# The second mixer's stick-breaking attention in single steps with stacked operands, and later turns at post-norms

## The chip, the cores and the metric

One Trainium2 chip, one of its cores. The metric is the device time of one execution in microseconds (us), as the median of the runs. On this kernel about 0.2% (7 us) can be told from no change.

## What is computed

A model of 512 tokens by 1024 features runs through two stacks in fp32. The first has two layers of a mixer (differential attention, retention, pooling) and a convolutional MLP; each result is normalised by a gain of its own ("post-norm") before it is added to x. The second has two layers of a gated MLP, a hybrid mixer (dilated windows and a stick-breaking attention) and another gated MLP. The parts that matter here:

```
x = x + rms_norm(mix, norm_mix_post[l]); h = rms_norm(x, norm_mlp_pre[l])   # post-norm
x = x + rms_norm(y, norm_mlp_post[l])                                       # post-norm

# stick-breaking attention, four heads of 64, q scaled by 1/8
z = q . k                                  # 512 x 512 a head, only keys before the query
log_keep = log_sigmoid(-z) = -softplus(z)
after = sum of log_keep over keys between this one and the query
o = exp(log_sigmoid(z) + after) . v

# dilated windows: 12 heads in 3 groups (dilation 1, 4, 16), rotary on q and k
```

## The kernel before

**Dense products.** Every weight is read from HBM in chunks of 128 x 1024 (`Stream`), split by ScalarE and VectorE into a high and a low fp32r part (L63, L64), and each product is three fp32r matmuls: high by high, high by low, low by high (`mm3a`, `mm3b`, L177 to L185). `fm` makes features by tokens, one 128 x 512 bank a chunk (24 matmuls); `tm` makes tokens by features in four banks at once, one for each tile of 128 tokens. With `halves`, `fm` first runs four chunks over tokens 0 to 255 and then over 256 to 511.

**Order by hand.** The program is emitted in one fixed order for each engine. Every dense step calls `tick`, which moves a clock on by 640 for three matmuls of 512 columns; the clock counts planned nanoseconds, not real ones. Three kinds of other work are put in by that clock. `later` queues steps of the norms with a due time and a token tile; `flush(t)` forces those of tiles up to t (an infinite due time leaves a step to that alone). `after` queues splits of rotated rows. `bg` holds generators (`stick`, then `dilated(0)`, then `dilated(1)`): each runs to its next `yield n` and then waits for n more ticks. `drain` runs what is left of them at once. Each engine takes its own instructions strictly in the order of emission, so one that waits holds up all behind it.

**Post-norms.** `finish` runs the last product of a stage in two halves of features. For a post-norm, `part1` (L340 to L358) takes ScalarE's square sum of a bank, multiplies the bank by its gain on VectorE (L347), makes the scale on GpSimd; `add`, 1200 ticks later, adds both halves to x (L354); then square sums of x, `rows_of_h` (2300 ticks later) scales x to xn on VectorE (L210), and `to_h` turns xn on TensorE into banks ph (L220) and splits them to h (L162, L163). `to_h` is due 1800 ticks after that, but for the last token tile, which waits for `flush`: in `fm` with halves at the start of the second half, in the first product of mix1 (`opens`) before tile t.

**Second mixer** (`mix2`, twice). In order: four half-run chunks make sq0, sk0, sq1, sk1 (two heads each); a `tm` makes v; six chunks q0, q2, q4, k0, k2, k4, each rotated (`rope`, L499 to L502: VectorE shuffle, VectorE multiply, GpSimd multiply, GpSimd add) and split 4500 ticks later; a second `tm` for the other v; six more chunks q1 to k5; sixteen gate chunks, with `drain` behind the twelfth. `stick` starts with the first `tm` and is followed by the two `dilated`, which wait for their names and 2500 ticks past the newest split. `stick` works on one head at a time: a mask and the scores into three banks z (plain fp32 matmuls on 64 rows, L1139 and L1140), softplus of the four blocks (three ScalarE functions, L1145 to L1147, and one VectorE step, L1148), splits, prefix sums over the keys by fp32r matmuls with triangles of -1 (`neg_tri`, L1157) and of blocks by all -1, exponentials, and the product with v (`pos`). Every helper `mm` records its matmuls at L1121. Its temporary tiles come from 9 buffers (`scr`), other features from 24 (`fm`).

Of the kernel before, what the change touches and what calls it, by code (L numbers as in the profile page):

```python
# [91 lines left out]
class Block:  # L92
# [225 lines left out]
    def finish(self, nk, rows, gain, scale=None, post=None, final=False):  # L318
# [21 lines left out]
        def part1(t, ps):  # L340
# [5 lines left out]
            self.square_sum(ys[t][:, 1:2], ps)  # L346
            nc.vector.tensor_mul(ps, ps, post[:, 512:])  # L347
            nc.gpsimd.tensor_add(ys[t][:, 2:3], ys[t][:, 0:1], ys[t][:, 1:2])
            self.rstd(ys[t][:, 3:4], ys[t][:, 2:3], D)

            def add():
                for n, src in ((0, y0[t]), (1, ps)):
                    x = self.X[:, t, n * 512:(n + 1) * 512]
                    nc.vector.scalar_tensor_tensor(x, src, ys[t][:, 3:4], x, op0=OP.mult, op1=OP.add)  # L354

                def sums():
                    self.x_ready(t, 0, ss[t])
                    normed(t)  # L358

                self.later(1900, t, sums)  # L360
# [3 lines left out]
        def normed(t):  # L364
# [3 lines left out]
            def rows_of_h():  # L368
                parts = self.scaled_rows(t, r, gain)
                if final:  # L370
                    for n in range(2):
                        nc.sync.dma_start(self.out[0, t * 128:(t + 1) * 128, n * 512:(n + 1) * 512], parts[n])
                else:
                    self.later(1800 if t < NT - 1 else math.inf, t, lambda: self.to_h(t, parts, first))

# [486 lines left out]
    def mix2(self, l, next_gain, final):  # L862
# [21 lines left out]
        def dil(name):  # L884
# [6 lines left out]
            def evac(ps):  # L891
# [3 lines left out]
                def split():  # L895
# [3 lines left out]
                    fm["at"] = self.clock  # L899
                self.after(4500, split)  # L900
            return evac
# [82 lines left out]
    def dilated(self, half, fm, v, o_dil):  # L984
# [6 lines left out]
        while any(n not in fm for n in names):  # L991
            yield 300
        while self.clock < fm["at"] + 2500 and not self.forced:
            yield 300
# [124 lines left out]
    def stick(self, fm, v, o_sb):  # L1119
# [4 lines left out]

        def split(x):
            n = x.shape[-1]
            hi = part()
            lo = hi[:, n:2 * n] if 2 * n <= T else part()[:, :n]
            self.split_to(hi[:, :n], lo, x)
            return hi[:, :n], lo  # L1130

        for h in range(4):
            c, s = divmod(h, 2)
            p = slice(64 * s, 64 * s + 64)
            q, k = fm[f"sq{c}"][p], fm[f"sk{c}"][p]
            banks = [self.bank(self.bg_tag, "pz") for _ in range(3)]
            z = [banks[0], banks[1][:, :384], banks[2][:, :256], banks[2][:, 256:384]]
            for b in range(NT):
                mm(z[b][:, :128], self.ident_bf, self.strict_kq, b < 3)  # L1139
                mm(z[b], k[:, b * 128:(b + 1) * 128], q[:, b * 128:], False)  # L1140
            x0, x1, x2 = [self.spare(f"sp{i}") for i in range(3)]
            sp = [x0, x1[:, :384], x2[:, :256], x1[:, 384:]]
            for b in range(NT):
                x = sp[b]
                nc.scalar.activation(x, z[b], AF.Abs)  # L1145
                nc.scalar.activation(x, x, AF.Exp, scale=-1.0)
                nc.scalar.activation(x, x, AF.Ln, bias=1.0)  # L1147
                nc.vector.scalar_tensor_tensor(x, z[b], 0.0, x, op0=OP.max, op1=OP.add)  # L1148
            yield 4500 if h else 6000
            parts = [split(sp[0]), split(sp[1]), split(sp[2])]  # L1150
            nc.vector.tensor_add(sp[2][:, 128:], sp[2][:, 128:], sp[3])
            nc.vector.tensor_add(sp[1][:, 128:], sp[1][:, 128:], sp[2])
            past = [split(sp[1]), split(sp[2])]
            yield 3500
            for b in range(3):
                for x in parts[b]:
                    mm(z[b], self.neg_tri, x, False)  # L1157
            mm(z[2][:, 128:], self.neg_ones.bitcast(F32), sp[3], False)
            mm(z[3], self.neg_tri.bitcast(F32), sp[3], False)
            yield 1000  # L1160
# [4 lines left out]
            for b in range(NT):  # L1165
# [3 lines left out]
                w.append(x[:, :n])  # L1169
            yield 4000  # L1170
            while ("v", NT - 1) not in fm:
# [158 lines left out]
```

## Time and profile before

| | us |
|---|---|
| median of 3 runs | 3435.41 |
| lowest, highest | 3434.85, 3436.55 |
| the profiled execution | 3436.64 |
| its span, first to last instruction | 3434.9 |
| TensorE busy (matmuls) | 3352.0 |
| VectorE busy | 1542.0 |
| ScalarE busy | 1192.8 |
| GpSimd busy | 356.3 |

The profile is of one execution. A matmul's end is modelled and overlaps the next one's start, so the distance from start to start tells what a matmul costs; busy time tells only that TensorE was not idle. The idle time in front of an instruction stands in square brackets in the timeline, with what ended it. The granted clock of TensorE (PEclk) is 1.00 at 2.4 GHz and 0.50 at 1.2 GHz; a window that is a little wider than a half-speed stretch shows 0.51.

### The profile page before, as it was taken

The numbers are of one execution on the slowest core, as the hardware profiler recorded it, in microseconds if no ns is written. First come the engines' busy times: TensorE is split into PE (matmuls) and PEld (weight loads), VectorE is DVE, ScalarE is ACT, GpSimd is POOL, SyncE is SP. The second block draws the span as 40 slices with busy tenths as digits, with TensorE's granted clock in tenths as the row PEclk, the third lists the DMA queues.
The fourth block names the chain that finished last, engine by engine and source line by source line (L and its number), as shares of the span: only waits on it lengthen the run. The fifth ranks groups of instructions, "written<-read, shape, count | busy, mean of one in ns | idle before, by whom it ended". The sixth has DMA issues, their size and how long they took to land.

```text
span 3434.9 us, 39516 instructions
## 1 busy us (share of the span) xinstructions
PE 3352.0 (98%) x16080; PEld 2770.5 (81%) x16080; DVE 1542.0 (45%) x2013; ACT 1192.8 (35%) x1886; POOL 356.3 (10%) x412
## 2 busy tenths in 40 slices
PE   8999999999999999999999999999999999999999
PEld 6778888767888888888688888888888878888887
DVE  4665542466555243323564533324332457453332
ACT  4344432434443232223533332223222443432222
POOL 2421110242110000000220100000000022010000
PEclk9999999999999999999999999999999999999999
DMA  4122332312233222232112232322232212223232
GB/s 158 49 75 86 104 112 92 108 50 75 86 105 111 92 93 96 95 104 97 59 64 77 90 103 95 104 92 97 95 104 98 96 51 68 82 91 103 94 103 80
DMA packets 87190, 311.99 MB, mean 91 GB/s; under 512 B 10368, under 2 KB 11072, under 8 KB 87008
## 3 DMA queue, kind: packets, MB, share of 16 engines
q1 hardware_dynamic: 85536, 305.17, 26.6%
q0 software_dynamic: 1472, 4.30, 0.4%
q8 instruction: 127, 2.08, 0.2%
q14 instruction: 55, 0.45, 0.0%
HBM read 307.32 MB, written 2.10 MB: 90 GB/s over the span
## 4 chain that ended last, share of the span: by engine, by line
PE 87%; DVE 6%; ACT 3%; POOL 2%; issue 2%; DMA 1%; DVEq 0%; POOLq 0%; ACTq 0%; SPq 0%
PE pa L177 17%; PE pa L178 17%; PE pa L179 17%; PE pb L183 10%; PE pb L184 10%; PE pb L185 10%; DVE wlo L64 1%; PE pz L1121 1%; PE ph L220 1%; PE pos L1121 1%; DVE xn L210 1%; PE pst L986 1%; DVE sh L499 1%; ACT whi L63 0%; PE psc L662 0%
## 5 line engine op out<-in xcount | busy, mean ns | idle before, releaser
L64 DVE TENSOR_TENSOR wlo<-wraw,whi 128x1024 fp32r<-128x1024 f32 x556 | 710.5, 1279 | 1113.1 <-ACT whi L63 1112.0
L177 PE MATMUL pa<-h_hi,whi 128*128 128x512 f32 (+1 forms) x3072 | 1164.5, 379 | 2.0 <-ACT h_hi L162 2.0
L178 PE MATMUL pa<-h_lo,whi 128*128 128x512 f32 (+1 forms) x3072 | 1145.3, 373 | 2.7 <-DVE h_lo L163 2.7
L179 PE MATMUL pa<-h_hi,wlo 128*128 128x512 f32 (+1 forms) x3072 | 1144.5, 373 | 0.0
L63 ACT ACTIVATE whi<-wraw 128x1024 fp32r<-128x1024 f32 x556 | 585.2, 1053 | 635.7 <-PE pb L185 540.7
L177 PEld LDWEIGHTS pa<-h_hi,whi 128*128 128x128 f32 x3072 | 580.5, 189 | 107.6 <-issue 4.9
L179 PEld LDWEIGHTS pa<-h_hi,wlo 128*128 128x128 f32 x3072 | 580.1, 189 | 101.3
L178 PEld LDWEIGHTS pa<-h_lo,whi 128*128 128x128 f32 x3072 | 581.0, 189 | 99.3 <-DVE h_lo L163 4.3
L183 PE MATMUL pb<-whi,hid_hi 128*128 128x512 f32 x1056 | 411.8, 390 | 0.0
L184 PE MATMUL pb<-wlo,hid_hi 128*128 128x512 f32 x1056 | 410.9, 389 | 0.0
L185 PE MATMUL pb<-whi,hid_lo 128*128 128x512 f32 x1056 | 410.9, 389 | 0.0
L183 PEld LDWEIGHTS pb<-whi,hid_hi 128*128 128x128 f32 x1056 | 198.2, 188 | 41.2
L185 PEld LDWEIGHTS pb<-whi,hid_lo 128*128 128x128 f32 x1056 | 198.2, 188 | 41.1
L184 PEld LDWEIGHTS pb<-wlo,hid_hi 128*128 128x128 f32 x1056 | 198.2, 188 | 40.7
L438 ACT ACTIVATE hid_hi<-act 128x512 fp32r<-128x512 f32 x88 | 55.6, 632 | 383.9 <-DVE act L449 383.9
L201 POOL TENSOR_TENSOR rs<-ss 128x1 f32<-128x1 f32 x44 | 12.0, 273 | 1601.8 <-ACT sqs L191 1601.8
L449 DVE TENSOR_TENSOR act<-act,pa 128x512 f32<-128x512 f32 x88 | 60.5, 687 | 210.3 <-PE pa L179 210.3
L458 DVE SCALAR_TENSOR_TENSOR cv<-pa,cw,cv 128x511 f32<-128x511 f32 (+1 forms) x176 | 131.5, 747 | 15.9 <-ACT cv L456 12.8
L445 ACT ACTIVATE act<-pa 128x512 f32<-128x512 f32 x88 | 52.5, 597 | 246.6 <-PE pa L179 246.6
L183 PE MATMUL pb<-whi,h_hi 128*128 128x512 f32 x256 | 108.0, 422 | 11.4 <-DVE fmraw L500 6.7
L184 PE MATMUL pb<-wlo,h_hi 128*128 128x512 f32 x256 | 102.9, 402 | 1.2 <-DVE wlo L64 1.2
L185 PE MATMUL pb<-whi,h_lo 128*128 128x512 f32 x256 | 102.7, 401 | 0.0
(323 smaller groups left out, 2934.5 us busy)
## 6 DMA issues: line engine op xcount, KB each, us to landing
wraw<-w_ffn SPq DMA_DIRECT2D x264, 512.0 KB, 3.2
wraw<-w_mix SPq DMA_DIRECT2D x160, 512.0 KB, 3.3
wraw<-w_mlp SPq DMA_DIRECT2D x132, 512.0 KB, 3.3
X<-x SPq DMA_DIRECT2D x4, 512.0 KB, 7.6
gain<-norm_ffn SPq DMA_DIRECT2D x4, 512.0 KB, 5.3
out<-xn SPq DMA_DIRECT2D x8, 256.0 KB, 2.0
gain<-norm_mix_pre SPq DMA_DIRECT2D x2, 512.0 KB, 5.5
rope_da<-c_rope SPq DMA_DIRECT2D x2, 512.0 KB, 8.4
```

Of the source, the lines that this page charges most:

```text
L63: self.nc.scalar.activation(hi, t, AF.Copy)
L64: self.nc.vector.tensor_sub(lo, t, hi.bitcast(F32))
L177: mm(ps, w[0], h[0], start=first, stop=False)
L178: mm(ps, w[0], h[1], start=False, stop=False)
L179: mm(ps, w[1], h[0], start=False, stop=last)
L183: mm(ps, h[0], w[0], start=first, stop=False)
L184: mm(ps, h[0], w[1], start=False, stop=False)
L185: mm(ps, h[1], w[0], start=False, stop=last)
L438: nc.scalar.activation(hid[0][:, f], h, AF.Copy)
L449: nc.vector.tensor_mul(g, g, ps)
L458: nc.vector.scalar_tensor_tensor(c[:, s:], ps[:, :T - s], cw[:, j, i:i + 1], c[:, s:], op0=OP.mult, op1=OP.add)
L1121: mm = lambda out, lhsT, rhs, first: nc.tensor.matmul(out, lhsT, rhs, start=first, stop=True, skip_group_check=True)
```

## The change

- At post-norms, tiles 2 and 3 both wait for `flush` with their turn (before: tile 3 alone); the gain's multiply of the second half moves from `part1` to the front of `add`.
- A rotated row's split comes 5500 ticks after its evacuation (4500), and `dilated` starts 4500 ticks after the newest split (2500).
- `stick`: queries and keys of a head are split into high and low fp32r parts. `both` holds the key's high part on the head's 64 rows and its low part on the other 64; the query's high part and its low part each stand on both halves. Two fp32r matmuls on 128 rows then give all four products, in place of one plain fp32 matmul on 64 rows. This is done for the next head before the v product of this one.
- The softplus of each block is a step of its own, with 1200 ticks between ScalarE's three functions and VectorE's step. Splits put ScalarE's copies 1300 ticks ahead of VectorE's subtractions. The last block's sums use its split parts in place of plain fp32. A head's yields add up to 17800 ticks in place of 14000.

```diff
@@ -344,11 +344,11 @@
                 normed(t)
                 return
             self.square_sum(ys[t][:, 1:2], ps)
-            nc.vector.tensor_mul(ps, ps, post[:, 512:])
             nc.gpsimd.tensor_add(ys[t][:, 2:3], ys[t][:, 0:1], ys[t][:, 1:2])
             self.rstd(ys[t][:, 3:4], ys[t][:, 2:3], D)
 
             def add():
+                nc.vector.tensor_mul(ps, ps, post[:, 512:])
                 for n, src in ((0, y0[t]), (1, ps)):
                     x = self.X[:, t, n * 512:(n + 1) * 512]
                     nc.vector.scalar_tensor_tensor(x, src, ys[t][:, 3:4], x, op0=OP.mult, op1=OP.add)
@@ -371,7 +371,8 @@
                     for n in range(2):
                         nc.sync.dma_start(self.out[0, t * 128:(t + 1) * 128, n * 512:(n + 1) * 512], parts[n])
                 else:
-                    self.later(1800 if t < NT - 1 else math.inf, t, lambda: self.to_h(t, parts, first))
+                    inside = t < (2 if post is not None else NT - 1)
+                    self.later(1800 if inside else math.inf, t, lambda: self.to_h(t, parts, first))
 
             self.later(2300, t, rows_of_h)
 
@@ -897,7 +898,7 @@
                     self.split_to(*[grouped(x) for x in parts], turned(raw))
                     fm[name] = parts
                     fm["at"] = self.clock
-                self.after(4500, split)
+                self.after(5500, split)
             return evac
 
         def gate(j):
@@ -990,7 +991,7 @@
         pair = self.window_kq[:, None, :].to_broadcast([128, 2, 256])
         while any(n not in fm for n in names):
             yield 300
-        while self.clock < fm["at"] + 2500 and not self.forced:
+        while self.clock < fm["at"] + 4500 and not self.forced:
             yield 300
         mx = [self.small.tile([128, 3, 4], F32, name="mx", bufs=2) for _ in range(2)]
 
@@ -1122,41 +1123,72 @@
                                                             skip_group_check=True)
         part = lambda: self.phase.tile([128, T], F32R, name="ab", tag="scr", bufs=self.n_scr)
 
-        def split(x):
-            n = x.shape[-1]
-            hi = part()
-            lo = hi[:, n:2 * n] if 2 * n <= T else part()[:, :n]
-            self.split_to(hi[:, :n], lo, x)
-            return hi[:, :n], lo
-
+        def split(xs):
+
+
+            got = []
+            for x in xs:
+                n = x.shape[-1]
+                hi = part()
+                nc.scalar.activation(hi[:, :n], x, AF.Copy)
+                got.append((hi[:, :n], hi[:, n:2 * n] if 2 * n <= T else part()[:, :n]))
+            yield 1300
+            for x, (hi, lo) in zip(xs, got):
+                nc.vector.tensor_sub(lo, x, hi.bitcast(F32))
+            return got
+
+        def stacked(h, wait):
+
+
+            c, s = divmod(h, 2)
+            p, other = slice(64 * s, 64 * s + 64), slice(64 - 64 * s, 128 - 64 * s)
+            q, k = fm[f"sq{c}"][p], fm[f"sk{c}"][p]
+            qh, ql, both = part(), part(), part()
+            for to in (p, other):
+                nc.scalar.activation(qh[to], q, AF.Copy)
+            nc.scalar.activation(both[p], k, AF.Copy)
+            yield wait
+            for to in (p, other):
+                nc.vector.tensor_sub(ql[to], q, qh[p].bitcast(F32))
+            nc.vector.tensor_sub(both[other], k, both[p].bitcast(F32))
+            return both, (qh, ql)
+
+        ready = yield from stacked(0, 1500)
+        yield 2500
         for h in range(4):
             c, s = divmod(h, 2)
             p = slice(64 * s, 64 * s + 64)
-            q, k = fm[f"sq{c}"][p], fm[f"sk{c}"][p]
+            k, qs = ready
             banks = [self.bank(self.bg_tag, "pz") for _ in range(3)]
             z = [banks[0], banks[1][:, :384], banks[2][:, :256], banks[2][:, 256:384]]
             for b in range(NT):
                 mm(z[b][:, :128], self.ident_bf, self.strict_kq, b < 3)
-                mm(z[b], k[:, b * 128:(b + 1) * 128], q[:, b * 128:], False)
+                for q in qs:
+                    mm(z[b], k[:, b * 128:(b + 1) * 128], q[:, b * 128:], False)
             x0, x1, x2 = [self.spare(f"sp{i}") for i in range(3)]
             sp = [x0, x1[:, :384], x2[:, :256], x1[:, 384:]]
+            yield 700
             for b in range(NT):
                 x = sp[b]
                 nc.scalar.activation(x, z[b], AF.Abs)
                 nc.scalar.activation(x, x, AF.Exp, scale=-1.0)
                 nc.scalar.activation(x, x, AF.Ln, bias=1.0)
+                yield 1200
                 nc.vector.scalar_tensor_tensor(x, z[b], 0.0, x, op0=OP.max, op1=OP.add)
-            yield 4500 if h else 6000
-            parts = [split(sp[0]), split(sp[1]), split(sp[2])]
+            yield 600
+            parts = yield from split([sp[0], x1, sp[2]])
+            parts.append([x[:, 384:] for x in parts[1]])
+            parts[1] = [x[:, :384] for x in parts[1]]
             nc.vector.tensor_add(sp[2][:, 128:], sp[2][:, 128:], sp[3])
             nc.vector.tensor_add(sp[1][:, 128:], sp[1][:, 128:], sp[2])
-            past = [split(sp[1]), split(sp[2])]
-            yield 3500
-            for b in range(3):
+            yield 1300
+            past = yield from split([sp[1], sp[2]])
+            yield 1300
+            for b in range(NT):
                 for x in parts[b]:
                     mm(z[b], self.neg_tri, x, False)
-            mm(z[2][:, 128:], self.neg_ones.bitcast(F32), sp[3], False)
-            mm(z[3], self.neg_tri.bitcast(F32), sp[3], False)
+            for x in parts[3]:
+                mm(z[2][:, 128:], self.neg_ones, x, False)
             yield 1000
             for b in range(2):
                 for x in past[b]:
@@ -1167,7 +1199,10 @@
                 x = self.scratch("sw")
                 nc.scalar.activation(x[:, :n], z[b], AF.Exp)
                 w.append(x[:, :n])
-            yield 4000
+            yield 1500
+            if h < 3:
+                ready = yield from stacked(h + 1, 1500)
+            yield 1500
             while ("v", NT - 1) not in fm:
                 yield 300
             if s == 0:
```

## Rows read from the trace of the kernel before

**Rows 1.** The page: busy time by engine, and the costliest group (mean ns of one).
```profile
PE 3352.0 (98%) x16080; PEld 2770.5 (81%) x16080; DVE 1542.0 (45%) x2013; ACT 1192.8 (35%) x1886; POOL 356.3 (10%) x412
...
L64 DVE TENSOR_TENSOR wlo<-wraw,whi 128x1024 fp32r<-128x1024 f32 x556 | 710.5, 1279 | 1113.1 <-ACT whi L63 1112.0
```

**Rows 2.** Who TensorE waited for: us in total, times, longest us.
```profile
PE ph L220 <- DVE xn L210: 20.5, 5, 8.2
PE pb L183 <- DVE fmraw L500: 6.7, 2, 3.3
...
PE pst L986 <- ACT fmk5h L162: 3.6, 2, 1.8
...
PE ph L220 <- DVE X L354: 1.6, 4, 0.4
...
PE pst L986 <- DVE fmk5l L163: 1.3, 2, 0.7
...
PE pz L1121 <- DVE ab L163: 1.2, 4, 0.5
PE pst L986 <- DVE fmk3l L163: 1.2, 2, 0.6
```

**Rows 3.** Windows, TensorE: us, busy (instructions), granted clock, DMA share, GB/s.
```profile
249.43:252.84 3.41, 3.36 (x16) 0.51 0.59 203
...
1792.20:1799.10 6.90, 6.25 (x36) 0.51 0.23 84
```

**Rows 4.** The same view of a stretch of dense matmuls, 512 columns each.
```profile
1842.00:1884.00 42.00, 42.00 (x187) 1.00 0.28 93
```

**Rows 5.** Timeline, TensorE, first mix1 into mlp1: start, us, what [idle before].
```profile
243.16 0.39 PE L185 MATMUL pb<-whi,mix_lo 128*128 128x512 f32 x1
249.48 1.97 PE L220 MATMUL ph<-ident,xn 128*128 128x128 f32 x8 [3.06 <-DVE xn L210]
...
262.62 0.39 PE L178 MATMUL pa<-h_lo,whi 128*128 128x256 f32 x1 [0.34 <-DVE h_lo L163]
```

**Rows 6.** Timeline, VectorE, the same place.
```profile
248.08 0.69 DVE L347 TENSOR_TENSOR pb<-pb,gain 128x512 f32<-128x512 f32 x1
...
254.66 1.41 DVE L210 SCALAR_TENSOR_TENSOR xn<-X,rs,gain 128x512 f32<-128x512 f32 x2 [1.85 <-POOL rs L168]
```

**Rows 7.** Timeline, TensorE, stick's first head: scores, then prefix sums.
```profile
1609.52 0.23 PE L1121 MATMUL pz<-masks 128*128 128x128 bf16 x1
1609.68 1.12 PE L1121 MATMUL pz<-fmsq,fmsk 64*128 64x512 f32 x2
...
1613.10 0.49 PE L183 MATMUL pb<-whi,h_hi 128*128 128x512 f32 x1
1613.43 0.39 PE L184 MATMUL pb<-wlo,h_hi 128*128 128x512 f32 x1
...
1622.76 1.20 PE L1121 MATMUL pz<-ab,tri 128*128 128x512 f32 x6
1623.80 0.61 PE L1121 MATMUL pz<-sp,tri 128*128 128x128 f32 x4
```

**Rows 8.** Timeline, VectorE and TensorE, the second v product of mix2.
```profile
1697.10 1.06 DVE L163 TENSOR_TENSOR fmk2l<-fmraw,fmk2h 128x512 fp32r<-128x512 f32 x1 [0.68 <-ACT fmk2h L162]
...
1698.08 0.73 DVE L499 STREAM_SHUFFLE sh<-pa 128x512 f32<-128x512 f32 x1
...
1699.43 0.63 PE L183 MATMUL pb<-whi,h_hi 128*128 128x512 f32 x1 [3.34 <-DVE fmraw L500]
```

**Rows 9.** Timeline, VectorE and GpSimd, the second batch of rotated rows.
```profile
1779.92 0.73 DVE L499 STREAM_SHUFFLE sh<-pa 128x512 f32<-128x512 f32 x1
...
1782.17 2.15 POOL L502 TENSOR_TENSOR fmraw<-fmraw,sh 128x512 f32<-128x512 f32 x1
...
1786.49 0.73 DVE L499 STREAM_SHUFFLE sh<-pa 128x512 f32<-128x512 f32 x1
```

**Rows 10.** Window of the first batch: busy of PE, PEld, DVE, ACT, POOL, then clock.
```profile
1640.00:1694.00 54.00, 53.38 (x222) 36.34 (x221) 32.81 (x49) 29.82 (x60) 17.16 (x10) 1.00 0.18 59
```

## The prediction

> **What bounds the kernel now.** The page first: TensorE's matmuls cover 98% of the span [rows 1]. So two things can give time: fewer or cheaper matmuls, and stretches in which TensorE waits. Second view: who TensorE waited for [rows 2]. Three of its waits lie where this change works. "ph from xn" is the turning of normed rows into columns: 20.5 us in five waits, of which 8.2 are the kernel's start, so 12.3 us in the four post-norms (one shown below). "pb from fmraw" is a bank that a rotated key still holds, 3.3 us in each mix2. "pst from fmk3l, fmk5h, fmk5l" is `dilated` scoring keys not yet split, 1.2 + 3.6 + 1.3 us over both mix2. Third view: the granted clock. Seven stretches right behind such waits run at half speed (1.2 in place of 2.4 GHz), at 249, 621, 850, 1700, 1792 (6.9 us long), 2806 and 2901 us, the others some 3.4 us each; first and longest are shown [rows 3]. They follow waits of 2 us and more, though not every such wait is followed by one (one of the four turns is not).
>
> A clock for the steps: dense work ticks 640 for three matmuls, and 185 whole ones in 42 us are 0.227 us each [rows 4], so 640 ticks are 0.68 us and 1000 ticks 1.06 us. Work that `stick` and `dilated` put in comes on top.
>
> **Post-norms: later turns, later multiply.** Before, row tile 2 is turned 1800 ticks after its scaling is queued; TensorE stands 3.06 us there because scaling xn(2) queues on VectorE behind the multiply L347 of tile 3, which waits for ScalarE's square sum [rows 5, 6]. After, tiles 2 and 3 turn where their columns are first needed: for mlp1 and ffn1 behind four half blocks, 96 matmuls of 256 columns at half of 0.227, 10.9 us after the stage opens at 243.4 [rows 5]; for the second mix1 behind two blocks of 24, 10.9 us too. xn(2) is ready by then (TensorE had it at 249.48), and xn(3), begun at 254.66 [rows 6] and no longer behind the copies of tile 2, meets TensorE at about 255: no wait, or up to 1 us. Removed: 12.3 us, and three half-speed stretches of 3.4 us, half of each, 5.1 us. Added: both tiles are copied and split when they are needed. One tile's splits cost TensorE 0.34 us before the second matmul behind them [rows 5] and, by my estimate, as much before the first; the second tile adds about 0.6 at each of four places, 2.4 us (0 to 5). Moving L347 into `add` takes it from in front of xn(t-1), so the bank that the first turn waits for, 1.6 us in four waits [rows 2], comes 0.6 us sooner. Sum: 12.3 + 5.1 + 1.6 - 2.4 = **16.6 us** (10 to 19).
>
> **Stick's scores.** Before, one head's scores hold TensorE from 1609.52 to 1613.10, 3.58 us: four masks of 0.16 and plain fp32 products that each run as two slow halves (1.05 us for 512 columns); the next dense matmul then takes 0.33 in place of 0.227 [rows 7]. After: the same masks, 0.64 us, and for every block two fp32r products on 128 rows. Six such of 512, 384 and 256 columns take 1.04 us (1622.76 to 1623.80); for the pair of 128 columns I take 2 x 0.09 to 0.11 from the four behind them (0.36 us) [rows 7]. Together 1.9 us: 1.7 saved a head, and 0.1 twice a head for the slow matmul behind fp32, since the last block's fp32 pair goes too. Eight heads: **15 us** (10 to 17).
>
> **The bank at the second v product.** Before, all four softplus blocks are queued at once; key k2's split stands behind them on ScalarE and VectorE (which waits 0.68 us for ScalarE and then takes 1.06), and k4's shuffle behind that. It starts at 1698.08, TensorE has waited 3.34 us when it is done, and runs at half speed then [rows 8]. After, head 2 of the stick is at its prefix sums there: the splits and adds of its parts were queued 1300 ticks and more earlier, and `stick` queues no softplus before tick 58100 (its scores for head 3 come at 57400 instead of 50400). The shuffle then starts within about a microsecond. Removed 2 x (3.3 + 1.7); I keep 0.3 each: **9.4 us** (5 to 10).
>
> **Dilated's second half.** Before, shuffle to shuffle is 6.57 us (1779.92 to 1786.49) where a dense block is 24 x 0.227 = 5.45: the split of key j is queued 4500 ticks after its evacuation, ahead of shuffle j+1 at 5120, and waits for GpSimd's part of the rotation, whose last step takes 2.15 us [rows 9]. The lateness adds up until k5. At 5500 ticks the split is queued behind shuffle j+1, so the loop opens; and `dilated` starts 4500 instead of 2500 ticks after the last split, 3000 later in all. Removed: 6.1 us of waits [rows 2] and half of 6.9 + 3.4 us of clock, some of it idle anyway: **10 us** (6 to 11). Each raw tile lives 1000 ticks longer, two at a time: at my count 18 of 24 buffers then.
>
> **What the steps cost.** A head's yields rise from 14000 to 17800 ticks, but head 0 waits for v at tick 20480 as before, so head 1 starts at 21800 (22100 before), and `stick` ends at 73700 instead of 64400, 9.9 us later. The first `dilated` starts at 73700, before the second batch's first split at 82560; the second starts at 112960 (110080), ends near 147000, and the drain is at 163840: nothing of it is on the path. Stacking adds per head three ScalarE copies and three VectorE subtractions, 64 rows by 512, which no row shows; I price a subtraction as one of 128 rows, 0.69 to 1.06 us [rows 6, 8]. VectorE was busy 32.8 of 54 us in that stage [rows 10]; 1.4 heads there add 4.6. But one block's shuffle (0.73 [rows 9]), its multiply of the same size, weight split (1.28 [rows 1]) and key split (1.06) hold it 3.8 us without a wait, and two steps of the new order fall right behind such a burst: head 1's second subtractions (queued at tick 31800, used at 34100) and the stacking for head 2 (queued at 37100, used at 39600). Each has about 2.5 us of cover, and TensorE's own work of the head there, about 2 us, against 3.8 and its own 2 us: some 1 us late, twice per mix2: **4 us** lost (0 to 12). The waits for the subtractions that the old yields left too short, 1.2 us [rows 2], go.
>
> The Trainium skill, "SBUF — State Buffer", section "Who interferes with whom", says that a VectorE instruction with two SBUF inputs and a GpSimd one that reads SBUF exclude each other, and the later one is blocked for the whole of the other. The trace agrees in kind (1.06 where 0.69 is usual, while GpSimd works), and it is the rule that speaks against adding such subtractions here; its sum is the second rival's.
>
> **Sum.** 16.6 + 15 + 9.4 + 10 + 1.2 - 4 = 48 us. The profiled execution took 3436.64 (span 3434.9 and 1.7 around it): 3388.4. The median of the three runs is 1.2 lower, so **3387 us**.
>
> **Rivals.**
> (1) Turns gain nothing: xn(3) arrives late, and two tiles' splits in a row cost what the wait did. For it: two banks and four copies in a row. Against: 11 us of dense work lie ahead of them. 3387 + 15 = 3402.
> (2) The stacked subtractions are blocked behind GpSimd's 2.15 us: each takes 2.84, three take 8.5 instead of 3.2, at one head per mix2 without cover: 3387 + 11 = 3398. For it: the 1.06 of k2's split. Against: GpSimd is busy 17 of 54 us [rows 10].
> (3) The first `dilated` misses its start. Every split sets its due time anew each 5120 ticks, and 4500 plus the tick's grain never fits between; it would then start at 112960 and the second at 147000, 17000 ticks of it behind the drain without cover: 18 us a layer, a third of it TensorE's own work. 3387 + 24 = 3411. It decides if `stick` ends 8900 ticks later than I count.
> (4) The change doesn't do what it says: k4's shuffle and k5's split still come late behind other queued work, so 19.4 us stay: 3406.
> (5) Slower than before: the 6.57 us loop of evacuation, GpSimd, split and next evacuation stays closed on VectorE, and stick's 3.5 us per block join it. Then a block takes 10.1 us against TensorE's 6.6, 3.5 us on 24 blocks: 3387 + 84 = 3471. It decides when VectorE's work per block passes 6.6 us, against 4.1 in 6.9 now; the split's new place speaks against it.
>
> **Chances.** Forecast 0.64; (1) 0.09; (2) 0.08; (3) 0.05; (4) 0.10; (5) 0.04. The range 3373 to 3407 takes in the bounds of the terms and rivals 1, 2 and 4. 0.2% (7 us) is about what a measurement tells from no change. Everything but (5) is faster by more; mixtures of several losses I put at 0.02 for the same: faster 0.94, same 0.02, slower 0.04.
>
> **What would show it.** In TensorE's waits after: "ph from xn" down to the start's 8.2 us, "pb from fmraw" and the three "pst" gone; the half-speed stretches of mix2 (four) and of the post-norms (three) gone; a head's scores 1.9 us; new waits of pz on the subtractions "ab" under 1 us each. Wrong if scores take over 2.5 us, if waits at the turns reappear on h_hi, or if pz waits on "ab" exceed 10 us.

## The result and the profile after

The changed kernel takes 3397.85 us (median of four runs, 3394.68 to 3400.86), the kernel before 3435.98 in the same series (3434.85 to 3437.65). The ratio is 0.9887, 95% interval 0.9874 to 0.9899: faster by 38 us. The forecast was 3387.0, range 3373 to 3407, so the direction and the range held and the time is 10.9 us above the forecast. The profiled execution took 3394.68, 42.0 less than the profiled one of before. The changed kernel's other three runs lie 1.5 to 6.2 us above its profiled one, with a granted clock of 0.993 to 0.994 where that one has 0.995; this makes most of the 3.9 us between the two differences.

The page of after first, busy time by engine (to [rows 1]), then who TensorE waited for (to [rows 2]; us in total, times, longest):

```profile
PE 3325.3 (98%) x16080; PEld 2760.9 (81%) x16080; DVE 1563.8 (46%) x2037; ACT 1207.0 (36%) x1910; POOL 361.4 (11%) x412
```

```profile
PE ph L220 <- DVE xn L210: 8.8, 1, 8.8
PE pz L1122 <- DVE ab L1137: 8.8, 4, 2.6
...
PE pa L178 <- DVE h_lo L163: 3.4, 8, 0.6
...
PE pa L177 <- ACT h_hi L162: 2.3, 8, 0.4
...
PE pz L1122 <- DVE ab L1153: 1.9, 2, 1.0
...
PE ph L220 <- DVE X L354: 0.3, 2, 0.2
```

TensorE's busy time fell by 26.7 us. Of the turning waits only the kernel's start is left (one wait, 8.8), "pb from fmraw" and all "pst" are gone. New are six waits of stick's products on its subtractions, 8.8 + 1.9 = 10.7 us in both second mixers, where before had 1.2.

By the signs that the prediction set itself, the removed waits and the turns came out as said, and one sign speaks against it: waits of stick's products on "ab" above 10 us were named as a sign of being wrong, and they are 10.7.

Where the 42.0 us went is read from the starts of the stages. TensorE's timeline, start of the first product of the second mixer of layer 1, and of the first product behind it whose rows are turned again; before, then after:

```profile
1596.58 0.38 PE L177 MATMUL pa<-h_hi,whi 128*128 128x256 f32 x1 [0.25 <-ACT h_hi L162]
...
1950.13 0.48 PE L183 MATMUL pb<-whi,fmyh 128*128 128x512 f32 x1
```

```profile
1579.16 0.38 PE L177 MATMUL pa<-h_hi,whi 128*128 128x256 f32 x1 [0.25 <-ACT h_hi L162]
...
1918.94 0.48 PE L183 MATMUL pb<-whi,fmyh 128*128 128x512 f32 x1
```

Up to the mixer 17.4 us are saved (1596.58 to 1579.16). The mixer's length goes from 353.55 to 339.78, 13.8 less; read in the same way, layer 2's goes from 352.18 to 341.12, 11.1 less. The feed-forward parts between and behind are unchanged within 0.3. So 17.4 for the post-norms and 24.9 for the two mixers.

The post-norm of [rows 5] after the change, TensorE:

```profile
243.48 0.39 PE L185 MATMUL pb<-whi,mix_lo 128*128 128x512 f32 x1
...
255.32 1.80 PE L220 MATMUL ph<-ident,xn 128*128 128x128 f32 x15
257.48 0.39 PE L177 MATMUL pa<-h_hi,whi 128*128 128x256 f32 x1 [0.36 <-ACT h_hi L162]
258.42 0.39 PE L178 MATMUL pa<-h_lo,whi 128*128 128x256 f32 x1 [0.56 <-DVE h_lo L163]
```

The wait of 3.06 and the half-speed stretch behind it are gone; the price is 0.36 + 0.56 where 0.34 stood. From the same product to the same product it is 14.94 us (243.48 to 258.42) where it was 19.46.

A head's scores after (to [rows 7]):

```profile
1596.16 0.23 PE L1122 MATMUL pz<-masks 128*128 128x128 bf16 x1
1596.20 0.71 PE L1122 MATMUL pz<-ab 128*128 128x512 f32 x2
...
1597.63 0.42 PE L1122 MATMUL pz<-ab 128*128 128x128 f32 x2
1597.89 0.45 PE L183 MATMUL pb<-whi,h_hi 128*128 128x512 f32 x1
```

They hold TensorE 1.73 us (1596.16 to 1597.89) in place of 3.58; a mask takes 0.04 to the next start where it took 0.16 ahead of plain fp32.

The three new waits of a mixer (TensorE's timeline: the second prefix sums of head 1, the scores of head 2, the prefix sums of head 2), and, as windows with the granted clock in the column behind the instructions, what followed them:

```profile
1639.95 0.72 PE L1122 MATMUL pz<-ab,tri 128*128 128x384 f32 x3 [1.79 <-DVE ab L1137]
...
1649.67 0.70 PE L1122 MATMUL pz<-ab 128*128 128x512 f32 x2 [0.95 <-DVE ab L1153]
...
1666.62 1.29 PE L1122 MATMUL pz<-ab,tri 128*128 128x512 f32 x3 [2.59 <-DVE ab L1137]
```

```profile
1666.90:1670.30 3.40, 3.40 (x13) 0.50 0.03 8
2759.10:2765.90 6.80, 6.53 (x20) 0.50 0.09 35
```

What VectorE did just ahead of the first and the last of them, and then what GpSimd did ahead of the first:

```profile
1637.67 1.75 DVE L163 TENSOR_TENSOR fmq0l<-fmraw,fmq0h 128x512 fp32r<-128x512 f32 x1
1639.35 0.88 DVE L1137 TENSOR_TENSOR ab<-sp,ab 128x384 fp32r<-128x384 f32 x2
...
1664.22 1.75 DVE L163 TENSOR_TENSOR fmk0l<-fmraw,fmk0h 128x512 fp32r<-128x512 f32 x1
1665.89 1.61 DVE L1137 TENSOR_TENSOR ab<-sp,ab 128x512 fp32r<-128x512 f32 x3
```

```profile
1636.75 2.13 POOL L503 TENSOR_TENSOR fmraw<-fmraw,sh 128x512 f32<-128x512 f32 x1
```

The split of a rotated row, moved to 5500 ticks, now stands right under GpSimd's addition for the next row and takes 1.75 us instead of 0.69 (in the groups of lines, five of the eight strided rows 2.14 to 2.20 instead of 1.05 to 1.12); stick's subtractions are queued behind it.

The kernel before had such holds too, on other instructions than the prediction read. VectorE there, in the first head with rotated rows beside it, then GpSimd:

```profile
1651.49 2.58 DVE L163 TENSOR_TENSOR ab<-sp,ab 128x512 fp32r<-128x512 f32 x3
```

```profile
1650.57 2.15 POOL L502 TENSOR_TENSOR fmraw<-fmraw,sh 128x512 f32<-128x512 f32 x1
...
1698.89 1.28 POOL L501 TENSOR_TENSOR sh<-sh,rope 128x512 f32<-128x512 f32 x1 [7.00 <-DVE sh L499]
```

Stick's three subtractions took 2.58 us there and take 1.61 after the change (1665.89 above); the mean of those on 512 columns is 1.50 and then 0.68. So the change moved the hold from stick's subtractions to the key splits. The second GpSimd line shows that GpSimd was idle for the 7.00 us before 1698.89, and key 2's split ran in these, at 1697.10 [rows 8].

### The profile page after: what moved, and what is told of

Same layout as the page of the kernel before. It is cut to its first block, busy times and chain, and to the rows that moved or that the text cites. A ratio compares the mean times of both kernels' runs of the same rounds, so it can differ in the third digit from the quotient of the medians.

```text
span 3392.9 us, 39523 instructions
## 1 busy us (share of the span) xinstructions
PE 3325.3 (98%) x16080; PEld 2760.9 (81%) x16080; DVE 1563.8 (46%) x2037; ACT 1207.0 (36%) x1910; POOL 361.4 (11%) x412
## 3 DMA queue, kind: packets, MB, share of 16 engines
q8 instruction: 127, 2.08, 0.3%
## 4 chain that ended last, share of the span: by engine, by line
PE 90%; DVE 5%; ACT 2%; POOL 2%; issue 1%; DMA 0%; DVEq 0%; POOLq 0%; ACTq 0%; SPq 0%
PE pa L177 18%; PE pa L178 18%; PE pa L179 18%; PE pb L183 10%; PE pb L184 10%; PE pb L185 10%; DVE wlo L64 1%; PE pz L1122 1%; PE ph L220 1%; PE pod L987 1%; PE pst L987 1%; ACT whi L63 1%; PE pos L1122 0%; DVE st L666 0%; PE psc L663 0%
```

## The experiments

Each is an edit of the changed kernel unless it says otherwise, on one core, with runs of the kernel before on the same chip beside it. They come from several series, in which the median of before lay between 3435.26 and 3437.42, and the intervals of two rows overlap when their medians are less than some 8 us apart: such a difference alone isn't shown. Where it matters, the lengths of the second mixers in the profiled executions are given as well, read as above: the two add up to 705.7 us before and to 680.9 in the changed kernel.

| run | median us | ratio to before (95%) | TensorE's waits that tell |
|---|---|---|---|
| changed kernel | 3397.85 | 0.9887 (0.9874 to 0.9899) | ab 10.7 |
| e1 split at 4500 | 3394.34 | 0.9880 (0.9866 to 0.9895) | ab 9.4, fmraw 1.3 |
| e2 split at 9400 | 3399.09 | 0.9890 (0.9874 to 0.9907) | ab 6.1, pst 3.8, pz on fmq2h 1.6 |
| e3 old turns | 3407.26 | 0.9919 (0.9905 to 0.9934) | xn 17.4, ab 8.8 at L1137 |
| e4 plain fp32 scores | 3406.76 | 0.9916 (0.9902 to 0.9931) | ab 8.5 |
| e5 multiply as before | 3396.19 | 0.9883 (0.9868 to 0.9898) | xn 8.3, ab 9.9 |
| e6 softplus in one go | 3398.31 | 0.9885 (0.9871 to 0.9900) | ab 13.6, no fmraw |
| e7 stick 10,000 ticks longer | 3429.83 | 0.9976 (0.9967 to 0.9986) | pst 14.3, pod 9.1, ab 10.7 |
| e8 before, with the due times of the rotated rows | 3422.53 | 0.9957 (0.9942 to 0.9972) | xn 20.9, fmraw 3.2, no pst |
| e9 more cover | 3392.83 | 0.9869 (0.9854 to 0.9883) | fmraw 5.9, pmt 3.3, no ab |
| e10 more cover and a gap | 3391.65 | 0.9870 (0.9854 to 0.9887) | fmraw 5.9, pmt 3.4, no ab |
| e11 rotation on VectorE | 3390.20 | 0.9864 (0.9849 to 0.9879) | ab 6.6 |
| e12 rotation on VectorE, more cover | 3378.49 | 0.9833 (0.9820 to 0.9847) | fmraw 1.7, no ab |

### Where the new waits come from: e1, e2, e4

My first theory was that the moved split, blocked by GpSimd, delays stick's subtractions; its rivals were that there is too little cover wherever the split stands, and that the stacking is simply too much work.

```diff
-                self.after(5500, split)
+                self.after(4500, split)
-        while self.clock < fm["at"] + 4500 and not self.forced:
+        while self.clock < fm["at"] + 5500 and not self.forced:
```

> The changed kernel with one thing undone: a rotated row's split is again queued 4500 ticks after its evacuation; the start of dilated stays where the change put it (5500 ticks behind the last split). Theory A (place): the changed kernel's waits of pz on the subtractions ab, 5.3 us in each mix2, come from key splits that now stand behind the next row's shuffle, right under GpSimd's rotation, where VectorE is blocked (1.75 to 2.19 us in place of 0.69); with the split ahead of the shuffle they fall to 3 us or less in both mix2 together, but the 6.57 us loop of the second batch comes back, with waits of pst on fmk5 only if the 3000 ticks don't cover it: 0 to 4 us. Time 3388 to 3396. Theory B (amount): the waits come from the added subtractions and steps themselves: they stay at 8 us or more, time 3397 to 3405.

The median is 3.5 us lower, with intervals that overlap, the two second mixers are no shorter (681.5 us), and the waits hardly fell (10.7 to 9.4, and 1.3 on fmraw). VectorE and then GpSimd in that run, the same place:

```profile
1633.37 0.68 DVE L163 TENSOR_TENSOR fmq0l<-fmraw,fmq0h 128x512 fp32r<-128x512 f32 x1
...
1637.15 1.95 DVE L1137 TENSOR_TENSOR ab<-sp,ab 128x384 fp32r<-128x384 f32 x2
...
1646.03 2.45 DVE L1152 TENSOR_TENSOR ab<-fmsq,ab 64x512 fp32r<-64x512 f32 x2
```

```profile
1636.23 2.12 POOL L503 TENSOR_TENSOR fmraw<-fmraw,sh 128x512 f32<-128x512 f32 x1
```

The split is back at 0.68, and GpSimd's hold has moved to whatever comes next: stick's second subtractions take 1.95 instead of 0.88, the stacked ones 2.45 instead of 1.37. So the instruction behind GpSimd's addition pays about 1.07 us, whether it is the split or a subtraction; the split's place chooses who pays. The waits are theory B's and the time is theory A's, so neither came out cleanly.

e2 puts the split at 9400 ticks and the start of `dilated` 900 after the last one (edit of the same two lines).

> The changed kernel with the split queued 9400 ticks after its evacuation, behind GpSimd's rotation of the next row, and dilated 900 ticks behind the last split, so that it starts at the same tick. Theory A (place): key splits take 0.7 us again, the waits of pz on ab fall from 10.7 us over both mix2 to 4 or less, time 3385 to 3392. Theory B (amount): the number of VectorE instructions in the batch is the same, so the waits stay at 8 us or more, time 3395 to 3401.

The waits on ab fall to 6.1, but the products that need the split rows now wait for them:

```profile
PE pz L1122 <- DVE ab L1137: 6.1, 4, 1.9
PE pst L987 <- ACT fmk3h L162: 2.5, 2, 1.3
PE pz L1122 <- ACT fmq2h L162: 1.6, 2, 0.8
PE pst L987 <- DVE fmk3l L163: 1.3, 2, 0.7
```

The key splits take 0.68 to 1.12 us again, the time is theory B's, and the waits on ab lie between the two theories. Nothing is gained by it. e4 takes the stacking out and scores from plain fp32 rows as before:

```diff
-            qh, ql, both = part(), part(), part()
...
             yield wait
...
-            return both, (qh, ql)
+            return k, (q,)
```

> The changed kernel without stacking: a head's scores are plain fp32 matmuls on 64 rows again, and the three copies and three subtractions of each head are gone; all yields stay. Prediction: 8 x 1.85 = 15 us for the scores come back; measured scores were 1.73 us a head, so 8 x 1.95 = 15.6. Theory A: of the waits of pz on VectorE only the one on the stacking itself (1.0 us in each mix2) goes: time 3409 to 3414. Theory B (the added subtractions make VectorE late): most of the 10.7 us go with them, and time is 3400 to 3406.

The waits at line 1137 stay (8.5 us in four), only the stacking's own, 1.9, go. So the stacking's own subtractions are not their cause, as theory A said; the time lies between the two theories' ranges. The stacked scores are worth 8.9 us net between the medians, and 12.4 in the profiled second mixers (693.3 us). Part of that is the clock. Both of e4's half-speed stretches in the second mixers (2697.0 and 2785.8 us) begin right behind a head's plain fp32 scores, with no wait of TensorE ahead; the first:

```profile
2696.51 0.49 PE L1122 MATMUL pz<-fmsq,fmsk 64*128 64x128 f32 x2
2696.93 0.75 PE L183 MATMUL pb<-whi,h_hi 128*128 128x512 f32 x1
2697.48 0.63 PE L184 MATMUL pb<-wlo,h_hi 128*128 128x512 f32 x1
```

### Post-norms: e3, e5

```diff
-                    inside = t < (2 if post is not None else NT - 1)
+                    inside = t < NT - 1
```

> The changed kernel with token tile 2 turned 1800 ticks after its scaling at post-norms, as before; the multiply stays in add. The prediction's term for the turns is 15 us without the multiply's share: four waits on xn of 2.5 to 3.2 us come back and some half-speed stretches behind them: 3409 to 3415, and 3408 or more if the multiply's new place shortens each wait by 0.7. The first rival (turns gain nothing, two tiles' splits in a row cost the same) expects 3396 to 3400.

The wait on xn comes back to 17.4 in five, and the half-speed stretches with it (247.6, 616.3, 848.4 and 1217.0 us), 9.4 us slower than the changed kernel between the medians. So the later turns are shown to gain, against the first rival, but by less than theory A's 3409 to 3415. In the profiled pair the second mixer opens at 1594.42 instead of 1579.16, 15.3 us later; 2.4 of it come back in the second mixers, which the edit doesn't touch (678.5 us), and another 3 us are that the changed kernel's profiled execution lies that much under its median.

```diff
             self.square_sum(ys[t][:, 1:2], ps)
+            nc.vector.tensor_mul(ps, ps, post[:, 512:])
...
             def add():
-                nc.vector.tensor_mul(ps, ps, post[:, 512:])
```

> The changed kernel with the multiply by the gain back where it was, ahead of the root and of the turns, and the turns as changed. Theory A: the multiply stood on the chain from the sum of squares to the first turn, so each of the places where the turns wait pays its 0.67 us and a little queueing, 2 to 4 us in all: 3399.5 to 3402, and the wait at a post-norm's end some 0.7 us longer than the changed kernel's. Rival B: with the turns placed later it has cover, within 1.5 us of the changed kernel, 3396 to 3399.5.

No difference that the medians can show (3396.19 against 3397.85): rival B's time. The waits show a small one: those of the first turns on the bank are back, as long as before the change [rows 2].

```profile
PE ph L220 <- DVE X L354: 1.5, 4, 0.4
```

The changed kernel has 0.3 in two there, so the multiply's new place takes 1.2 us of waits away also with the late turns. With the old turns it took more: xn is 20.5 before and 17.4 in e3, which keeps the multiply in `add`.

### What freed the bank: e6, e8

e6 takes the yield of 1200 out of the softplus loop and puts 4800 behind it.

> The changed kernel, but the softplus of a head's four blocks is queued in one go, as in the kernel before: no yield inside the loop, and the 4800 ticks taken out of it stand after it, so that every later step keeps its tick. Theory A (my prediction's): it was this queueing in one go that held VectorE and so the bank at the second value product; the wait on fmraw, which is gone in the changed kernel, comes back with 3 to 6.7 us in all, the time lies 3 to 9 us above the changed kernel's, at 3400 to 3407. Rival B: what freed that bank was that head 3's steps now lie some 7000 ticks later, beside other products; no wait on fmraw over 1 us, time 3394 to 3400.

No wait on fmraw returns and the time is the same (3398.31): rival B. The "single steps" of the softplus are not what frees the bank. They do something else: without them the waits on ab are 13.6 us in place of 10.7, and the second mixers are 4.3 us longer (685.2). That head 3's steps now lie 7000 ticks later is the cause that is left; no run moves head 3 back alone, and e1 and e8 show that the split's due time has a share in it.

e8 is the kernel before with the two due times of the rotated rows alone:

```diff
-                self.after(4500, split)
+                self.after(5500, split)
-        while self.clock < fm["at"] + 2500 and not self.forced:
+        while self.clock < fm["at"] + 4500 and not self.forced:
```

> The kernel before with one edit: the split of a rotated row 5500 ticks after its last product in place of 4500, and the start of dilated's scores 4500 ticks after the last row in place of 2500. Theory A: this edit alone removes the waits of the dilated part's second half (fmk3l, fmk3h, fmk5l, fmk5h, some 7 us of them); time 3424 to 3430. Rival B: it moves the splits against the next row's work only and new waits stand in their place; 3432 to 3438.

It saves 14 us, more than either theory said. All waits on fmk3 and fmk5 are gone, and so are the four half-speed stretches in the second mixers; a new one of 3.4 us at 2768.2 begins right behind a head's plain fp32 scores, as in e4. fmraw halves as well:

```profile
PE ph L220 <- DVE xn L210: 20.9, 5, 8.2
...
PE pb L183 <- DVE fmraw L500: 3.2, 2, 1.6
```

### The third rival's point and price: e7

```diff
-            yield 1000
+            yield 1000 if h < 3 else 11000
```

> The changed kernel, but the last step of the stick part ends 10,000 ticks later, which is more than the 8900 ticks that I read as its slack before the first dilated part misses its start. Theory A (the mechanism of the prediction's third rival): some of the dilated parts' work is left for the drain at the end of the mixer, where TensorE has nothing else; 8 to 12 us for each of the two mixers, 3412 to 3424. Rival B: the slack is larger than I read, or the late work still finds cover; within 3 us of the changed kernel, 3393 to 3401.

32 us slower than the changed kernel, beyond both theories. The first `dilated` starts scoring at 1748.6 instead of 1705.0, and the second's value products run in the drain (the second line below). The first line is another place: `dilated`'s third scores wait for a bank until VectorE, behind the splits of k3 and k5, has added a mask to the first. TensorE and then two windows:

```profile
1762.62 0.55 PE L987 MATMUL pst<-fmq0h,fmk0h 64*128 64x256 f32 x1 [7.15 <-DVE es L1031]
...
1845.88 0.58 PE L987 MATMUL pod<-es,v 128*128 128x128 f32 x1 [4.53 <-ACT es L1088]
```

```profile
1759.20:1769.40 10.20, 6.72 (x25) 0.50 0.31 103
1844.50:1851.30 6.80, 5.42 (x21) 0.50 0.23 80
```

That the first `dilated` misses its start and leaves work to the drain is as the rival had it. Its price of 24 us is near the two waits' 23.4 by luck: only 9.1 of them are in the drain, and the 14.3 at the scores it didn't have. The clock comes on top: in the stretches behind these waits TensorE works 12.1 us at half speed in layer 1 (the windows) and 9.9 in layer 2, 11 us lost in all.

### Cover, and GpSimd's hold: e9 to e12

e9 gives ticks where the three waits stand (e10 adds 2500 ahead of head 3):

```diff
             past = yield from split([sp[1], sp[2]])
-            yield 1300
+            yield (1300, 3300, 4000, 1300)[h]
...
                 ready = yield from stacked(h + 1, 1500)
-            yield 1500
+            yield 2700 if h == 1 else 1500
```

> The changed kernel with more ticks where its three new waits stand: 2000 more ahead of the sums of head 1, 2700 more ahead of those of head 2, 1200 more after the stacking for head 2; 5900 in all, under the 8900 ticks that I read as the slack of the stick part. Theory A: the waits are the price of too little cover, the work on VectorE behind them is unchanged; the waits on ab fall from 10.7 us to under 4 and the time to 3384 to 3392. Rival B: later steps meet the next blocks' ends and the waits move with them; waits on ab and pz 7 us or more, time 3393 to 3400.

The waits on ab are gone, all six, but the bank's wait is back, 5.9 us, and 3.3 of `dilated`'s maxima, so theory B is half right. The median is 5 us lower, with intervals that overlap. The second mixers are only 2.3 us shorter (678.6); in the profiled pair 2.9 more lie ahead of them, where the edit changes nothing. TensorE at the bank, and VectorE ahead of it:

```profile
1662.88 0.63 PE L183 MATMUL pb<-whi,h_hi 128*128 128x512 f32 x1 [2.96 <-DVE fmraw L501]
```

```profile
1658.67 0.29 DVE L1177 SCALAR_TENSOR_TENSOR sp<-pz,sp 128x128 f32<-128x128 f32 x1 [1.03 <-ACT sp L1175]
1659.19 1.63 DVE L1137 TENSOR_TENSOR ab<-sp,ab 128x512 fp32r<-128x512 f32 x3 [0.23 <-ACT ab L1133]
...
1661.53 0.73 DVE L500 STREAM_SHUFFLE sh<-pa 128x512 f32<-128x512 f32 x1
```

Subtractions of stick now stand ahead of the shuffle that empties the bank. I took them for head 3's and moved head 3:

> The changed kernel with the extra ticks of the run before (2000 ahead of the sums of head 1, 2700 ahead of those of head 2, 1200 after the stacking for head 2), and 2500 more ahead of head 3, 700 fewer behind it: 7700 in all, under the slack. Theory A: the wait on fmraw that came back there (3.0 us a mixer) is a meeting of head 3's subtractions with the end of a block of weights; 2500 ticks later they miss each other: fmraw under 1 us, the time 3 to 6 us under the run before, 3386 to 3390. Rival B: it meets another block's end or the dilated parts start too late: other waits of 3 us or more, 3391 to 3400.

Theory A fell: the wait stayed as it was (5.9) and the time too. They are head 2's, which e9 had moved 3200 ticks later and e10 does not move further.

e11 takes GpSimd out of the rotation of the second mixer's rows:

```diff
-        nc.gpsimd.tensor_mul(sh, sh, sin)
-        nc.gpsimd.tensor_add(out, out, sh)
+        on.tensor_mul(sh, sh, sin)
+        on.tensor_add(out, out, sh)
...
-                self.rope(raw, ps, self.ROPE16, rope[:, 0], rope[:, 1])
+                self.rope(raw, ps, self.ROPE16, rope[:, 0], rope[:, 1], nc.vector)
```

> The changed kernel with the two steps of a rotated row that GpSimd does (1.29 and 2.08 us) moved to VectorE, in the second mixer only: 24 rows, two more steps of some 0.68 us each there, and no GpSimd work beside VectorE at a block's end. Theory A: the splits that stand behind GpSimd's addition (1.75 to 2.20 us where they were 0.69 to 1.12) are what makes the waits on ab; they go back to 0.7 to 1.1 us, the waits of line 1137 fall from 8.8 to under 4 us and the time to 3386 to 3394. Rival B: VectorE's queue at the block's end is what counts, and it is as long as before (1.36 us more of its own work in place of some 1.1 to 1.8 us of standing still); waits on ab 7 us or more, 3394 to 3402.

VectorE, the place that showed 1.75 above, with its two new steps:

```profile
1663.51 0.68 DVE L503 TENSOR_TENSOR sh<-sh,rope 128x512 f32<-128x512 f32 x1
1664.23 0.69 DVE L504 TENSOR_TENSOR fmraw<-fmraw,sh 128x512 f32<-128x512 f32 x1
1664.84 1.22 DVE L64 TENSOR_TENSOR wlo<-wraw,whi 128x1024 fp32r<-128x1024 f32 x1
1665.97 0.69 DVE L163 TENSOR_TENSOR fmk0l<-fmraw,fmk0h 128x512 fp32r<-128x512 f32 x1
```

All splits are back at 0.68 to 1.12, and VectorE's busy time is 1561.0 us against 1563.8 although it does 48 more instructions: what it took over, it had been standing still for. The time is theory A's (3390.20, though its interval still meets the changed kernel's), the second mixers are 6.0 us shorter (674.9), and the waits lie between (6.6 us in place of 10.7). So 4.1 us of them were GpSimd's hold; the rest stands without any GpSimd work beside it, behind VectorE's queue at a block's end, and goes with more cover (e12).

e12 has both cures, with ticks for the two waits that e11 leaves:

```diff
-            yield 1300
+            yield (1300, 3300, 3100, 1300)[h]
```

> The changed kernel with both of the cures: the rotation of the second mixer's rows all on VectorE, and more ticks where the two waits on ab are left with it (1.9 and 1.55 us a mixer): 2000 more ahead of the sums of head 1, 1800 more ahead of those of head 2, 3800 in all. Theory A: cover and GpSimd's hold are two separate causes that add up; waits on ab under 2 us, no wait on fmraw or pmt over 1 us, 6 to 7 us under the run with the rotation alone, 3382 to 3387. Rival B: head 2's subtractions move ahead of a block's end and hold its bank, as in the two runs with more ticks: a wait on fmraw of 1 to 3 us a mixer, 3387 to 3392.

3378.49 us (3377.02 to 3380.97, five runs), better than any time of either theory, and faster than both kernels: 0.9833 (0.9820 to 0.9847). Its first waits:

```profile
PE ph L220 <- DVE xn L210: 8.5, 1, 8.5
...
PE pb L183 <- DVE fmraw L502: 1.7, 2, 0.9
```

No wait on ab is left, nor a half-speed stretch in the second mixers. Their lengths, read as above, are 333.54 and 333.57 us, 6.2 and 7.6 below the changed kernel's. In the profiled pair 2.5 us more lie ahead of the second mixer of layer 1: 1.0 in the first 17 us of the program, and most of the rest where the first mixer ran at half speed at 209.4 us in the changed kernel and not in this one. No edit touches that, so I don't count it.

## Why the prediction was right, and 10.9 us off

- **Post-norms, 16.6 us.** In the profiled pair it held: 17.4, all four waits and the three half-speed stretches gone, and 0.92 us of the split in place of 0.34. Between the medians e3 gives the turns only 9.4, where the prediction had 15 without the multiply. The multiply's share, 1.6 us of bank waits, is seen in the waits (1.2 in e5) and is below what the medians can show.
- **Stick's scores, 15 us.** Held: 1.85 us saved a head, 14.8 over eight. The fit is partly luck: the four masks take 0.15 us where 0.64 stood, and the four pairs 1.58 where 1.24 stood.
- **Bank, 9.4 us, and dilated's second half, 10 us.** The waits went entirely, 6.7 and 6.1 us, and with them all four half-speed stretches that were named. Their division was wrong: the due times of the rotated rows alone bring 14 us (e8), half of the bank's wait among it, and the softplus in single steps has no part in it (e6). What the prediction gave as its second reason, head 3 coming later, is the one that is left.
- **What the steps cost, 4 us: the mis-sized term.** It named two of the three places rightly, head 1's second subtractions and the stacking for head 2, and priced each at 1 us; they cost 1.79 and 0.95, and the sums of head 2, which it missed, 2.59: 5.3 a mixer, 10.7 us in all. Two half-speed stretches of 3.4 and 6.8 us follow them and cost half, 5.1; the term had nothing for the clock. Together 15.8 where 4 stood, past the end of its bounds, 12. Part of the error is the price of a key's split: the text took 1.06 us from a row of before for one that the same change moves under GpSimd's addition, where it takes 1.75 to 2.20. By e11 GpSimd's hold makes 4.1 of the 10.7 us of waits.
- **Rival 2.** Its time, 3398, is where the kernel came out, and this is partly luck as well. The Trainium skill, "SBUF — State Buffer", section "Who interferes with whom", has a VectorE instruction with two SBUF inputs and a GpSimd one that reads SBUF hold each other off. The trace agrees: the split at 1637.67 ends at 1639.42, 0.54 us after GpSimd's addition at 1638.88. The row that the prediction read for it doesn't show it: key 2's split took 1.06 us while GpSimd was idle. It is a strided row, and all strided splits of before took 1.05 to 1.12, the others 0.68 to 0.69. The rows that did show it were stick's own subtractions, 2.58 us. The prediction weighed the rule for the stacked subtractions only; in the changed kernel it struck the key splits, which the change moved, and in e1, with these moved back, stick's and the stacked subtractions.
- **The clock.** The prediction had half-speed stretches behind waits of 2 us and more. Two of its seven, at 1792 and 2901, follow waits of no more than 1.8 us, and those of e4 and e8 behind plain fp32 scores follow none.
- **Balance of the profiled pair.** 31.6 us were predicted for the mixers, 24.9 came: 11.8 more were lost on the steps, and some 5 more were gained elsewhere. Of these 5, about 2 are the bank's and `dilated`'s waits and stretches, which went whole (12.8 us of waits and 8.5 by the clock, where 19.4 stood); the rest wasn't traced. So the profiled pair is 6.2 us short of the forecast's 48.2; 3.9 more are the profiled pair against the medians, and the last 0.8 is mostly the median of before, 0.6 higher in this series.
- **Left open.** e12's gain of 13.8 us in the second mixers is about what the waits (10.7 gone, 1.7 new) and the clock (5.1) add up to, 14.1. Not tried: e12's smaller cover without the rotation on VectorE, so that both cures are needed is not shown; and why the first mixer has a stretch in some executions and not in others.

## What to carry to other kernels

When a change moves an instruction in a queue, price it by what will run beside it in its new place, not by a row from its old one, and ask the same of everything queued behind it. Where two engines hold each other off, moving an instruction may only pass the cost on: with the split at 4500, 5500 and 9400 ticks (e1, the changed kernel, e2) it went from one instruction to the next, and only leaving one of the two engines out (e11) took it away. And ticks of cover for one wait move all later steps against the block ends, so the waits are to be read again after each such edit (e9, e10, e12).

## What the runs showed of the hardware

The additions that GpSimd did in 2.08 us beside VectorE cost VectorE about as much standing still as doing them itself: 24 rows, two steps of 0.68 us more each, and 2.8 us less busy time in all. A bf16 mask product of 128 columns is followed by an fp32r one 0.04 us later, by a plain fp32 one only 0.16 later. A wait of TensorE of 2.6 us was followed by 3.4 us at half the clock in layer 1 and by 6.8 in layer 2, the same wait at the same place. Three stretches of 3.4 us at half the clock (two in e4, one in e8) began right behind a head's plain fp32 scores on 64 rows, 3.58 us long, without a wait.
